# Two-block network on one core: experts gather the unsplit h and sum in a tile apart, h g + b moves to the last eight experts, one more weight buffer, GpSimd products on VectorE

## Chip, cores and metric

One core of a Trainium2 chip runs the whole kernel. The metric is the device time of one execution in microseconds. The profiled execution is one of these executions.

## The reference

Two blocks of two layers each, on 256 tokens of width 1024, all in float32. The first block puts 16 meta tokens ahead of the 256 and has a gated linear recurrence in its first layer and a short convolution in its second; each is followed by a layer norm and by a mixture of 32 experts, of which every token takes two. The second block has a state space layer and an attention layer, each followed by a dense layer of width 4096.

```python
# layer i of the first block
mixed = rglru_mixer(h, ...) if i == 0 else shortconv_mixer(h, ...)
h = layer_norm(ALPHA * h + mixed, ln_g[i, 0], ln_b[i, 0])      # (x - mu) * rsqrt(var) * g + b
ffn = hierarchical_moe(h, ...)     # router: best of 4 groups, best two of its 8 experts, gates
h = layer_norm(ALPHA * h + ffn, ln_g[i, 1], ln_b[i, 1])
# one expert: (silu(x @ w_gate[e]) * (x @ w_up[e])) @ w_down[e], 1024 -> 512 -> 1024
```

The 32 experts of one layer hold 201 MB of weights, all of which are read.

## The kernel before

The 256 tokens live in two tiles `h[0]` and `h[1]` of 128 x 1024 (token on the partition). After a norm the tile holds only (x - mu) * rsqrt(var); the factor g (times ALPHA) and the summand b are applied later, in two ways: where a product needs h transposed, the transposed copy gets g and b per partition; and the tile itself becomes h g + b at a convenient point, before the next sum goes into it (`affine`, L362, `renew`, L368). `load_gb` (L429) fetches the next g and b: four rows of 2 KB with DMAs of GpSimd's queue into two scratch tiles of the pool `xk` (two buffers, also used by `hh` and `ht` of the experts), and four partition broadcasts on GpSimd.

Dense products run in float32r (one pass of TensorE): both operands are split into a high part (ScalarE copy, L294) and a low part (VectorE subtraction, L295), and three matmuls add up (L506 to L508). `feature_part` (L394) makes the split transposed copy of h for these products; of every two calls one is not "fast", and there the low part of a 128 x 512 tile is a GpSimd subtraction (L427). It is called for two tiles in `features` (layer 1 of the first block, state space layer) and for one tile at the end of three later stages, ten such subtractions in all.

`phase_a` (L566) is the first mixer. Its gates make a product `x * q` of 128 x 544 on GpSimd (L641, four times), and its scan a product of 128 x 272 on GpSimd before each `tensor_tensor_scan` (L688, eight times).

`moe` (L786) is the mixture. In this order of the program: router logits (L761, added at L855), `choose` (L801 to L849, some thirty small operations on VectorE that end in the one-hot tile `on`, L828, and later the gates), the ranks of the tokens by three small matmuls with a triangle and with ones (L880) into `rk`, the largest count (a register that all engines load, because an `If`, L1114, treats overfull experts apart), the places `P` (a 0/1 matrix of 128 tokens x 8 experts x 32 slots, L958), and the gather of eight experts at a time: `P` as the moving operand, h as the weights (L940, L941), to transposed inputs `xg`. For this h is split once (`xh` by ScalarE, `xl` by GpSimd, L865 and L866), four tiles of 128 x 1024, and each product takes two matmuls in float32r. After that split, GpSimd turns h into h g + b (`self.affine(self.gb, nc.gpsimd)`, L893) and loads the next g and b.

Then come eight quads of four experts. Each takes gate and up (L995, four experts beside each other in 32 columns of the array), silu on ScalarE (L1003), the multiply on VectorE (L1004), transposes (L1009), down (L1034), and the way back to the tokens (L1046), which VectorE adds to h (L1058). Every second quad gathers for two. The last quad adds and takes the moments of the norm at once.

Weights come through a ring of buffers of 1 MB each (`fetch`, L449, L462), filled by DMAs of SP's queue in program order; a DMA waits until its buffer has been read. In layer 0 the ring has 16 buffers up to the 33rd step of the stage generator, in layer 1 17 for the first two quads and 7 afterwards, because the tables of the state space layer are made beside the other six quads (`s5_prepare`, on all engines). The ring of 7 stays to the end.

The engines work in order each; the program is put into an order by a scheduler, except where an operation is pinned to the order of the program (`self.pin`).

```python
xh = [X.tile([128, KD, 128], F32R, name=f"xh{n}") for n in range(2)]
xl = [X.tile([128, KD, 128], F32R, name=f"xl{n}") for n in range(2)]
for n in range(2):
    src = h[n].rearrange("t (p k) -> t k p", k=KD)
    self.pin(a.copy)(xh[n], src)
    nc.gpsimd.tensor_tensor(xl[n], src, xh[n].bitcast(F32), op=OP.subtract)
```

## Time and profile before

| | us |
|---|---|
| median of 3 runs | 1877.05 (1873.78 to 1881.48) |
| profiled execution, its own time | 1877.19 |
| its span, first to last instruction | 1875.5 |
| TensorE matmuls busy | 1562.1 (83%) |
| VectorE busy | 855.2 (46%) |
| ScalarE busy | 508.0 (27%) |
| GpSimd busy | 177.5 (9%) |

The mean granted clock of TensorE is 0.932 of 2.4 GHz. The kernel reads 526 MB from memory, 281 GB/s over the span. The shares are averages over stages with different limits; a stage is read from its own stretch. An operation's busy time includes the time in which it waits inside the engine for something that is no semaphore.

### The profile page before, as it was taken

The numbers are of one execution on the slowest core, as the hardware profiler recorded it, in microseconds if no ns is written. First come the engines' busy times: TensorE is split into PE (matmuls) and PEld (weight loads), VectorE is DVE, ScalarE is ACT, GpSimd is POOL, SyncE is SP. The second block draws the span as 40 slices with busy tenths as digits, with TensorE's granted clock in tenths as the row PEclk, the third lists the DMA queues.
The fourth block names the chain that finished last, engine by engine and source line by source line (L and its number), as shares of the span: only waits on it lengthen the run. The fifth ranks groups of instructions, "written<-read, shape, count | busy, mean of one in ns | idle before, by whom it ended". The sixth has DMA issues, their size and how long they took to land.

```text
span 1875.5 us, 24906 instructions
## 1 busy us (share of the span) xinstructions
PE 1562.1 (83%) x10036; PEld 996.9 (53%) x10044; DVE 855.2 (46%) x1752; ACT 508.0 (27%) x811; POOL 177.5 (9%) x235
## 2 busy tenths in 40 slices
PE   7878677777777997876787778768999999999997
PEld 6764222211222894221132233247989998879997
DVE  5873111201111966111441342178775657885655
ACT  4631000100000542110010010033554445654442
POOL 3331000000000403001000000012110100310100
PEclk9878989988999998998898899878999999999999
DMA  9356999999999863999999899995745543435530
GB/s 308 141 215 273 420 420 420 420 420 420 419 420 387 305 236 146 421 415 397 399 380 379 339 390 404 357 190 158 248 136 180 188 160 115 167 113 180 180 135 23
DMA packets 150520, 535.56 MB, mean 286 GB/s; under 512 B 23141, under 2 KB 35686, under 8 KB 120698
## 3 DMA queue, kind: packets, MB, share of 16 engines
q1 hardware_dynamic: 148226, 532.04, 75.2%
q0 software_dynamic: 1856, 1.75, 0.4%
q8 instruction: 81, 1.33, 0.3%
q14 instruction: 45, 0.37, 0.1%
q10 hardware_dynamic: 312, 0.07, 0.0%
HBM read 526.49 MB, written 1.05 MB: 281 GB/s over the span
## 4 chain that ended last, share of the span: by engine, by line
PE 35%; DMA 14%; DVE 7%; ACT 2%; POOL 1%; issue 1%; SPq 0%; DVEq 0%; ACTq 0%; POOLq 0%
DMA raw<-in_moe_w_up 9%; PE mm L507 5%; PE mm L506 5%; PE mm L508 5%; PE tp L507 3%; PE tp L506 3%; PE tp L508 3%; DMA raw<-in_moe_w_gate 3%; PE mm L1034 3%; PE mm L995 3%; DMA raw<-in_moe_w_down 2%; PE tp L1449 1%; PE mm L1046 1%; PE mm L1521 1%; DVE hc L1567 0%
## 5 line engine op out<-in xcount | busy, mean ns | idle before, releaser
L995 PE MATMUL mm<-raw,xg 128*32 128x512 f32 x2048 | 381.3, 690 | 164.1 <-DMA raw<-in_moe_w_up 93.1
L295 DVE TENSOR_TENSOR wlo<-raw,whi 128x1024 fp32r<-128x1024 f32 (+3 forms) x265 | 283.7, 1086 | 170.2 <-ACT whi L294 169.5
L995 PEld LDWEIGHTS mm<-raw,xg 128*32 128x32 f32 x2048 | 80.7, 121 | 448.1 <-DMA raw<-in_moe_w_up 170.5
L294 ACT CAST whi<-raw 128x1024 fp32r<-128x1024 f32 (+3 forms) x265 | 239.0, 917 | 245.3 <-PE mm L508 100.1
L1004 DVE TENSOR_TENSOR hh<-hh,mm 128x512 f32<-128x512 f32 x16 | 11.0, 688 | 470.3 <-PE mm L995 470.3
L1034 PE MATMUL mm<-raw,ht 128*32 128x512 f32 (+2 forms) x1120 | 208.6, 604 | 17.0 <-DMA raw<-in_moe_w_down 12.1
L506 PE MATMUL mm<-whi,f 128*128 128x512 f32 (+3 forms) x432 | 150.0, 347 | 0.0
L507 PE MATMUL tp<-f,whi 128*128 128x256 f32 x512 | 146.4, 286 | 4.2 <-DVE f L423 4.2
L507 PE MATMUL mm<-wlo,f 128*128 128x512 f32 (+3 forms) x432 | 149.8, 347 | 0.0
L508 PE MATMUL mm<-whi,f 128*128 128x512 f32 (+3 forms) x432 | 149.1, 346 | 0.0
L506 PE MATMUL tp<-f,whi 128*128 128x256 f32 x512 | 146.3, 286 | 0.4 <-ACT f L417 0.4
L508 PE MATMUL tp<-f,wlo 128*128 128x256 f32 x512 | 146.1, 286 | 0.0
L1034 PEld LDWEIGHTS mm<-raw,ht 128*32 128x32 f32 x1120 | 53.7, 118 | 129.5 <-issue 84.9
L1003 ACT ACTIVATE hh<-mm 128x512 f32<-128x512 f32 x16 | 9.6, 597 | 416.2 <-PE mm L995 416.1
L507 PEld LDWEIGHTS tp<-f,whi 128*128 128x128 f32 x512 | 99.7, 195 | 4.5 <-issue 4.5
L506 PEld LDWEIGHTS tp<-f,whi 128*128 128x128 f32 x512 | 99.5, 195 | 1.3 <-ACT f L417 0.9
L508 PEld LDWEIGHTS tp<-f,wlo 128*128 128x128 f32 x512 | 99.8, 195 | 0.0
L507 PE MATMUL mm<-xl,whi 128*128 128x272 f32 (+2 forms) x320 | 93.1, 292 | 0.8 <-DVE xl L295 0.4
L506 PE MATMUL mm<-xh,whi 128*128 128x272 f32 (+2 forms) x320 | 92.8, 295 | 0.6 <-ACT yg L678 0.4
L508 PE MATMUL mm<-xh,wlo 128*128 128x272 f32 (+2 forms) x320 | 92.1, 289 | 0.0
L506 PEld LDWEIGHTS mm<-whi,f 128*128 128x128 f32 x432 | 81.8, 189 | 10.3
L508 PEld LDWEIGHTS mm<-whi,f 128*128 128x128 f32 x432 | 81.5, 189 | 10.1 <-DVE f L423 0.2
(615 smaller groups left out, 2425.5 us busy)
## 6 DMA issues: line engine op xcount, KB each, us to landing
raw<-in_moe_w_gate SPq DMA_DIRECT2D x128, 1024.0 KB, 12.3
raw<-in_moe_w_up SPq DMA_DIRECT2D x128, 1024.0 KB, 19.9
raw<-in_moe_w_down SPq DMA_DIRECT2D x120, 1024.0 KB, 19.0
raw<-in_w_ff SPq DMA_DIRECT2D x64, 1024.0 KB, 4.9
raw<-in_sc_w_in SPq DMA_DIRECT2D x12, 1024.0 KB, 12.4
raw<-in_lru_w_in SPq DMA_DIRECT2D x8, 1024.0 KB, 13.8
raw<-in_ssm_w_glu SPq DMA_DIRECT2D x8, 1024.0 KB, 10.5
raw<-in_moe_w_down SPq DMA_DIRECT2D x12, 512.0 KB, 13.3
```

What stands on the lines that cost most here:

```text
L294: f(self.nc.scalar.copy)(hi, src)
L295: f(self.nc.vector.tensor_tensor)(lo, src, hi.bitcast(F32), op=OP.subtract)
L506: mm(out, lhsT=lh, rhs=rh, start=first, stop=False, skip_group_check=shared)
L507: mm(out, lhsT=lh, rhs=rl, start=False, stop=False, skip_group_check=shared)
L508: mm(out, lhsT=ll, rhs=rh, start=False, stop=last, skip_group_check=shared)
L995: nc.tensor.matmul(gu[m][i * 32:(i + 1) * 32, :], lhsT=xg[hf][:, k, c], rhs=wgu[hf * n + part][m][i][:, k % (4 // n), :], start=hf == 0 an ...
L1003: a.activation(hh, gu[0], AF.Silu)
L1004: v.tensor_tensor(hh, hh, gu[1], op=OP.mult)
L1034: nc.tensor.matmul(o[e * 32:(e + 1) * 32, :], lhsT=ht[:, j, e * 32:(e + 1) * 32], rhs=w[e], start=j == 0, stop=j == 3)
L1046: nc.tensor.matmul(o, lhsT=pt[:, n, :], rhs=y[c.start // 512][j][:, c.start % 512:(c.stop - 1) % 512 + 1], start=j == 0, stop=j == 1)
L1449: nc.tensor.matmul(po[:, :, j:4, :], lhsT=sel[:, 67 - 64 * g - j:195 - 64 * g - j], rhs=Kg[:, g, :, 0:4 - j, :], start=n == 0, stop=n == 7)
L1521: nc.tensor.matmul(p, lhsT=self.place[:, 128 * q4 + 3 - j:128 * q4 + 131 - j], rhs=x[:, :, 64 * j:64 * j + 64], start=j + i == 0, stop=j + ...
```

## The change

- The gather takes h itself (`hk`, a view of the tiles) in plain f32, one matmul instead of two; `xh` and `xl` are gone, with the copies and subtractions that made them, and `P` is f32.
- The experts' results are added into two new tiles `acc`, cleared by GpSimd at the start of `moe`, instead of into h. In quad 6, after its gate and up products are issued, `renew` turns h into h g + b on VectorE and loads the next g and b, and VectorE adds `acc` to h; quads 6 and 7 add to h as before.
- In layer 0 the router of the two meta rows (`lg2`, `choose`) and the cleared tile `yo` move behind the first gate and up products.
- The subtraction of `feature_part`, the gates' product and the scan's product go from GpSimd to VectorE.
- The ring has one buffer more: 17 instead of 16 in layer 0, 8 instead of 7 from the third quad of layer 1 on. Two places give room for it: the scan tiles `hc` of the state space layer use a second buffer of the ring, and the value tile `vv` of the attention is one.

```diff
     def renew(self, key, scale=None):
-        self.affine(self.gb)
+        for z in self.h:
+            for t, op in zip(self.gb, (OP.mult, OP.add)):
+                self.pin(self.nc.vector.tensor_tensor)(z, z, t, op=op)
         self.gb = self.load_gb(key, scale)
...
             a.copy(dst[0][:, s, o], y)
-            nc.gpsimd.tensor_tensor(dst[1][:, s, o], y, dst[0][:, s, o].bitcast(F32), op=OP.subtract)
+            v.tensor_tensor(dst[1][:, s, o], y, dst[0][:, s, o].bitcast(F32), op=OP.subtract)
...
-                    nc.gpsimd.tensor_tensor(x, x, q, op=OP.mult)
+                    v.tensor_tensor(x, x, q, op=OP.mult)
...
-                nc.gpsimd.tensor_tensor(x, x, tt[:, t, :], op=OP.mult)
+                v.tensor_tensor(x, x, tt[:, t, :], op=OP.mult)
...
+            acc = [X.tile([128, D], F32, name=f"acc{n}") for n in range(2)]
+            for t in acc:
+                nc.gpsimd.memset(t, 0.0)
...
-            xh = [X.tile([128, KD, 128], F32R, name=f"xh{n}") for n in range(2)]
-            xl = [X.tile([128, KD, 128], F32R, name=f"xl{n}") for n in range(2)]
-            for n in range(2):
-                src = h[n].rearrange("t (p k) -> t k p", k=KD)
-                self.pin(a.copy)(xh[n], src)
-                nc.gpsimd.tensor_tensor(xl[n], src, xh[n].bitcast(F32), op=OP.subtract)
...
-            self.affine(self.gb, nc.gpsimd)
-            self.gb = self.load_gb(("a", layer, 1))
...
+            hk = [t.rearrange("t (p k) -> t k p", k=KD) for t in h]
...
-                            nc.tensor.matmul(o, lhsT=xh[n][:, k, :], rhs=P[n], start=n == 0, stop=False)
-                            nc.tensor.matmul(o, lhsT=xl[n][:, k, :], rhs=P[n], start=False, stop=n == 1)
+                            nc.tensor.matmul(o, lhsT=hk[n][:, k, :], rhs=P[n], start=n == 0, stop=n == 1)
...
-                    t = B.tile([128, 8, 32], F32R, name=f"P{n}")
+                    t = B.tile([128, 8, 32], F32, name=f"P{n}")
...
+                if qd == 6:
+
+                    self.renew(("a", layer, 1))
+                    for n in range(2):
+                        v.tensor_tensor(h[n], h[n], acc[n], op=OP.add)
+                    acc = h
                 if N == 3 and qd == 0:
+                    lg2 = S.tile([2, 1, 36], F32, name="lg2")
+                    v.tensor_tensor(lg2[:, 0, :], self.logits(layer, self.x2[:, 0]), self.br[layer][:2, :], op=OP.add)
+                    gt2 = choose(lg2, "2")[1]()
...
-                            v.tensor_tensor(h[n][:, c], h[n][:, c], back(n, c), op=OP.add)
+                            v.tensor_tensor(acc[n][:, c], acc[n][:, c], back(n, c), op=OP.add)
...
-            t = self.fetch(None, [128, 4, 8, 64])
+            t, u = (self.fetch(None, [128, 4, 8, 64]) for _ in range(2))
...
-                hcs.append([keep.tile([128, 8, 64], F32, name=f"hc{i}{n}") if i else t[:, 2 + n] for n in range(2)])
+                hcs.append([keep.tile([128, 8, 64], F32, name=f"hc{n}") if i == 3 else (t[:, 2:], u, u[:, 2:])[i][:, n] for n in range(2)])
...
-            vv = P.tile([128, 2, NH, 128], F32, name="vv")
+            vv = self.fetch(None, [128, 2, NH, 128])
...
         self.shrink()
-        self.grow(1)
+        self.grow(2)
...
         self.grow(4, AT)
-        self.grow(2)
+        self.grow(3)
         self.moe(0, [128, 128, 2], self.stages0())
```

The loop over overfull experts adds to `acc` in the same way; it isn't entered with these inputs.

## Rows read from the trace of the kernel before

**Rows 1.** Windows view: stretch in us, busy us by engine, granted clock, DMA share, GB/s

```profile
80.00:92.00 12.00, 4.80 (x12) 3.26 (x13) 9.54 (x17) 9.56 (x17) 8.31 (x6) 0.61 0.01 1
140.00:158.00 18.00, 14.09 (x99) 7.88 (x104) 11.42 (x63) 2.82 (x5) 4.22 (x6) 0.79 0.16 51
160.00:570.00 410.00, 312.14 (x1638) 97.77 (x1638) 59.67 (x129) 27.07 (x43) 0.95 (x1) 0.94 1.01 420
726.00:748.00 22.00, 12.62 (x77) 7.79 (x81) 12.94 (x33) 1.33 (x3) 11.14 (x8) 0.65 0.02 7
960.00:1170.00 210.00, 163.44 (x992) 61.28 (x994) 63.77 (x117) 19.41 (x32) 0.98 (x2) 0.92 0.97 375
1020.00:1060.00 40.00, 35.66 (x204) 14.55 (x202) 15.96 (x27) 3.79 (x6) 0.00 (x0) 0.93 0.83 291
```

**Rows 2.** Groups of VectorE by line, 125 to 139 us: busy us, mean ns

```profile
L811 DVE TENSOR_TENSOR goh<-goh,rev 128x8 f32<-128x8 f32 x1 | 2.8, 2786 | 0.0
L828 DVE TENSOR_TENSOR on<-oh,oh 128x64 f32<-128x64 f32 x1 | 2.2, 2246 | 0.0
L817 DVE TENSOR_TENSOR els<-lg,gof 128x64 f32<-128x64 f32 x1 | 2.2, 2244 | 0.0
L813 DVE TENSOR_TENSOR goh<-goh,gsm 128x8 f32<-128x8 f32 x1 | 2.1, 2066 | 0.0
L837 DVE TENSOR_TENSOR g<-m 128x2 f32<-128x2 f32 x1 | 1.6, 1629 | 0.0
L810 DVE TENSOR_TENSOR goh<-lg,gmx 128x8 f32<-128x8 f32 x1 | 1.2, 1191 | 0.0
...
L827 DVE TENSOR_TENSOR oh<-iota,i 128x64 f32<-128x64 f32 x1 | 0.2, 212 | 0.0
```

**Rows 3.** Timeline around the router of layer 0: start us, us

```profile
123.56 5.68 POOL L866 TENSOR_TENSOR xl<-h,xh 128x1024 fp32r<-128x1024 f32 x2 [31.89 <-ACT xh L96]
129.20 9.54 POOL L96 TENSOR_TENSOR h<-h,gb 128x1024 f32<-128x1024 f32 x4
152.11 0.15 DVE L810 TENSOR_TENSOR goh<-lg,gmx 2x4 f32<-2x4 f32 x1
```

**Rows 4.** Timeline of TensorE, layer 0, from the ranks to the first gate product

```profile
138.88 0.64 PE L880 MATMUL mm<-on,tri 128*128 128x32 f32 x2 [10.37 <-DVE on L828]
...
151.37 1.07 PE L995 MATMUL mm<-raw,xg 128*32 128x512 f32 x3
```

**Rows 5.** Timeline around the router of layer 1

```profile
719.64 2.44 DVE L810 TENSOR_TENSOR goh<-lg,gmx 128x8 f32<-128x8 f32 x1
732.22 2.25 DVE L828 TENSOR_TENSOR on<-oh,oh 128x64 f32<-128x64 f32 x1
```

**Rows 6.** Timeline of TensorE: split gather, and plain f32 products of the same shape

```profile
160.91 0.28 PE L940 MATMUL tp<-P,xh 128*128 128x256 f32 x1
...
161.14 0.28 PE L940 MATMUL tp<-P,xh 128*128 128x256 f32 x1
...
1631.57 0.59 PE L1873 MATMUL mm<-kz,qt 128*128 128x256 f32 x2
1632.00 0.59 PE L1896 MATMUL mm<-e,vv 128*128 128x256 f32 x2
```

**Rows 7.** First block: VectorE's wait (us in total, times, longest), and its scans

```profile
DVE rq L642 <- POOL xc L641: 4.9, 4, 1.2
...
71.99 2.43 DVE L689 TENSOR_TENSOR_SCAN tt<-rq,xc 128x272 f32<-128x272 f32 x2 [0.87 <-POOL xc L688]
92.24 1.33 DVE L689 TENSOR_TENSOR_SCAN tt<-rq,xc 128x272 f32<-128x272 f32 x2
```

**Rows 8.** Groups of GpSimd by line: the feature subtraction

```profile
L427 POOL TENSOR_TENSOR f<-xk,f 128x512 fp32r<-128x512 f32 x8 | 11.0, 1376 | 114.2 <-ACT f L426 84.9 <-issue 29.3
```

**Rows 9.** Groups by line: the experts' multiply with its idle time, the broadcast

```profile
L1004 DVE TENSOR_TENSOR hh<-hh,mm 128x512 f32<-128x512 f32 x16 | 11.0, 688 | 470.3 <-PE mm L995 470.3
L444 POOL PARTITION_BROADCAST gb<-gbr x32 | 38.8, 1303 | 205.6 <-DVE h L96 184.2 <-SPq L1114 12.1 <-ACT xh L294 8.3
```

More of the change, by code (lines that the diff above doesn't have):

```diff
@@ L360, in norm, with renew @@
         self.norm_end(small, n)
-    def affine(self, gb, e=None):
+    def renew(self, key, scale=None):
         for z in self.h:
-            for i, op in enumerate((OP.mult, OP.add)):
-                self.pin((e or self.nc.vector).tensor_tensor)(z, z, gb[i], op=op)
-    def renew(self, key, scale=None):
-        self.affine(self.gb)
+            for t, op in zip(self.gb, (OP.mult, OP.add)):
+                self.pin(self.nc.vector.tensor_tensor)(z, z, t, op=op)
         self.gb = self.load_gb(key, scale)
@@ L869, in moe @@
             logits(1)
+            next(two, None)
             if N == 2:
                 self.warm(WARMR)
-            next(two, None)
             on, gates = choose(lg, "")
@@ L969, in moe @@
             with self.pool("mz") as Z:
-                self.moe_rest(layer, S, B, Z, nc.values_load(most), counts, rk, gt, gather, cap)
-            if N == 3:
-                lg2 = S.tile([2, 1, 36], F32, name="lg2")
-                v.tensor_tensor(lg2[:, 0, :], self.logits(layer, self.x2[:, 0]), self.br[layer][:2, :], op=OP.add)
-                gt2 = choose(lg2, "2")[1]()
-                yo = X.tile([128, D], F32, name="yo")
-                nc.gpsimd.memset(yo, 0.0)
+                self.moe_rest(layer, S, B, Z, nc.values_load(most), counts, rk, gt, gather, cap, acc)
             for qd in range(8):
@@ L998, in moe @@
                         next(stages, None)
+                if qd == 6:
[3 more added lines that the diff above has]
+                    acc = h
                 if N == 3 and qd == 0:
+                    lg2 = S.tile([2, 1, 36], F32, name="lg2")
+                    v.tensor_tensor(lg2[:, 0, :], self.logits(layer, self.x2[:, 0]), self.br[layer][:2, :], op=OP.add)
+                    gt2 = choose(lg2, "2")[1]()
                     next(two)
                     affine2(1, *self.f_ln["a", layer, 0])
+                    yo = X.tile([128, D], F32, name="yo")
+                    nc.gpsimd.memset(yo, 0.0)
                 hh = self.scratch("hh")
@@ L1016, in moe @@
                 for n in range(2):
-                    nc.tensor.transpose(p[:, n * 128:(n + 1) * 128], P[n].bitcast(F32)[:, q], self.ident)
+                    nc.tensor.transpose(p[:, n * 128:(n + 1) * 128], P[n][:, q], self.ident)
                 o = p[:, 256:260]
                 for n in range(2):
-                    nc.tensor.matmul(o, lhsT=P[n].bitcast(F32)[:, q], rhs=gt[:, n, e0:e0 + 4], start=n == 0, stop=n == 1 and N == 2)
+                    nc.tensor.matmul(o, lhsT=P[n][:, q], rhs=gt[:, n, e0:e0 + 4], start=n == 0, stop=n == 1 and N == 2)
                 if N == 3:
@@ L1108, in most, with moe_rest @@
         return mi, counts
-    def moe_rest(self, layer, S, B, Z, most, counts, rk, gt, gather, cap):
-        nc, I, tc, h = self.nc, self.I, self.tc, self.h
+    def moe_rest(self, layer, S, B, Z, most, counts, rk, gt, gather, cap, acc):
+        nc, I, tc = self.nc, self.I, self.tc
         v, a = nc.vector, nc.scalar
@@ L1132, in chunk @@
                             v.tensor_scalar(s, re[:, n:n + 1], -cap - 64.0 * c, None, op0=OP.add)
-                            t = Z.tile([128, 64], F32R, name=f"P{n}")
+                            t = Z.tile([128, 64], F32, name=f"P{n}")
                             v.tensor_scalar(t, self.iota, s, None, op0=OP.is_equal)
                             g = Z.tile([128, 64], F32, name=f"Pg{n}")
-                            v.tensor_scalar(g, t.bitcast(F32), ge[:, n:n + 1], None, op0=OP.mult)
+                            v.tensor_scalar(g, t, ge[:, n:n + 1], None, op0=OP.mult)
                             q = self.bank("tp")
@@ L1167, in chunk @@
                                 nc.tensor.matmul(o, lhsT=pt[:, n, :], rhs=y[i], start=True, stop=True)
-                                v.tensor_tensor(h[n][:, cc], h[n][:, cc], o, op=OP.add)
+                                v.tensor_tensor(acc[n][:, cc], acc[n][:, cc], o, op=OP.add)
                     chunk(0)
```

## The prediction

> **What bounds the kernel now.** I read the windows view first. From 160 to 570 us, the expert loop of layer 0, the DMA engines are busy all the time at 420 GB/s while TensorE is busy 312 of 410 us [rows 1]: that stretch is paid by bytes, and only an earlier start of the stream, or more bytes ahead of it, shortens it. Then I looked for the places where the stream stands still. There are two holes in front of the expert loops, 140 to 158 us (DMA share 0.16) and 726 to 748 us (0.02) [rows 1]: all weight buffers are full and nothing is consumed yet, because the router has not chosen. A third stretch, 1020 to 1060 us, runs at 291 GB/s with TensorE busy 35.7 of 40 us [rows 1]; there TensorE is late. After 1205 us the dense blocks are bound by TensorE and the DMA doesn't matter.
>
> So the question is what fills the holes. The groups of VectorE in the router of layer 0 show six small two-input products, 128x2 to 128x64 elements, of 1191 to 2786 ns [rows 2]. The same line on a 2x4 tile, without a neighbour on GpSimd, takes 0.15 us [rows 3]. The timeline gives the cause: GpSimd runs two subtractions (5.68 us) and four products (9.54 us) at that time [rows 3], and each of the six ends where one of these ends. TensorE waits 10.37 us for the last of them [rows 4]. Layer 1 repeats it: six such products, the first 2.44 us, the last 2.25 us, the last ends at 734.47 [rows 5].
>
> **The sum.** It is made against the profiled execution: 1877.2 us, span 1875.5, its median neighbour 1877.05, so they can be taken as one. A measurement of this kernel tells about 0.5%, 9.4 us, from no change.
>
> *Router of layer 0.* The change takes away the ScalarE copies, the GpSimd subtractions and the four products from here. The six add up to 1191 + 2786 + 2066 + 2244 + 1629 + 2246 = 12.16 us [rows 2]; free, 6 x 0.18 = 1.1 us (between the 0.15 of the 2x4 product [rows 3] and the 0.21 of an unhindered 128x64 one [rows 2]). That is 11.1 us, but TensorE waited only 10.37 [rows 4], so 10.4. The partition broadcasts of the next g and b, 1.3 us each [rows 9], leave too, and the 2-row router moves behind the first gate and up products (about 1 us of TensorE and VectorE together). Against it stands the gather: unsplit, a pair of matmuls (high, low) becomes one. The pair starts every 161.14 - 160.91 = 0.23 us; an unsplit f32 product of the same 128x256 shape every 1632.00 - 1631.57 = 0.43 us [rows 6]. Half a gather is 8 of them: +1.6 us. Net 11 us; bounds 9 (nothing besides the six, gather wholly exposed) and 12.
>
> *One buffer more.* 128 x 2048 x 4 bytes = 1.05 MB, at 420 GB/s [rows 1] 2.5 us of stream that runs before the consumer comes. The hole of layer 0 is (1 - 0.16/1.01) x 18 = 15.1 us; 11 + 2.5 = 13.5 still fits into it, so both count. The Trainium skill (DMA: Bandwidth & Descriptors, Where 436 GB/s comes from) lets the memory side bind a load at about 358 GB/s; by that the buffer would be worth 2.9 us (an estimate from that figure), but the trace streams at 420 and the measurement decides.
>
> *Router of layer 1.* Six products at 13.4 us by the same pattern (the first and last are in [rows 5]), less 1.1: 12.3. The split gather ran 16 matmuls at 1.2 GHz here (granted clock 0.65 over the hole [rows 1]); an unsplit one at 2.4 GHz takes as long, 8 x 0.43 = 3.5 us, and at 1.2 GHz 7 us. I take 12; bounds 8.5 and 13. The hole, 22 us, is longer than that. The first eight experts have 17 buffers before and after; the new one comes only after them.
>
> *Inside layer 1.* From 960 to 1170 us the stream gives 375 GB/s [rows 1], against 420 a loss of 210 x 45/420 = 22 us, over half of it (40 x 129/420 = 12 us) in 1020 to 1060. Seven buffers become eight there: 2.5 us for each time the consumer falls behind, some four times at most, 10 us. But two of the later pairs of quads gather in this stretch, 2 x 2 halves x 1.6 = 6.4 us on an engine that is late. Bounds -6.4 and +10; +2, since where TensorE is busy 35.7 of 40 us a buffer pays once.
>
> *First block.* Four products 128x544 and eight 128x272 go from GpSimd to VectorE. VectorE waited 4.9 us for the former [rows 7], and its scans beside the latter took 2.43 us for two instead of 1.33 [rows 7]. On VectorE they cost about 0.7 us (a 128x512 product: 688 ns [rows 9]) and half of it: 4 x 0.72 + 8 x 0.4 = 6 us. Only 80 to 92 us counts, where TensorE is busy 4.8 of 12 us [rows 1]; half of the waits (2.5) and the scans' and subtractions' delay (some 2.5) lie there, and half of the new work (3). +2, bounds 0 and 3.5.
>
> *The ten feature subtractions* cost 1376 ns on GpSimd [rows 8], about 0.7 on VectorE [rows 9], each in front of a projection. But VectorE now waits in order for ScalarE's copy, and behind it stand the scaling of the next tile and its statistics, for which TensorE's transposes wait. +1 in all; bounds -2 and +4.
>
> *The quad before the last* (qd 6) takes over h g + b: four products and two sums of 128x1024, each at most twice 688 ns [rows 9], 8 us per layer on VectorE, in front of the multiply of gate and up. Before that multiply VectorE idles 470 us over 16 quads, 29 each [rows 9], so they cost nothing; without that cover, 8 us per layer. Behind them GpSimd loads the next g and b (four small DMAs of its own queue, four broadcasts of 1.3 us) into the two scratch buffers that the multiply and its transposed copy use next; that ends some 8 + 5 = 13 us after the last gather of the quad, still inside the 29. Clearing the two new sums is a GpSimd write before the router; nobody waits for it until the first sum. The GpSimd and SP queues have nothing else behind these steps. The shared scan buffers and the attention's value tile in the ring cost 0, between -1 and +4 (a buffer held longer).
>
> Sum: 11 + 2.5 + 12 + 2 + 2 + 1 = 30.5. 1877.2 - 30.5 = 1847 us, own range 1836 to 1858.
>
> **Rivals.** *Something else is late next* (0.17). With VectorE free, sixteen small matmuls of the meta rows, the branch that all engines pass before the loop, and a gather still at 1.2 GHz stand between router and first product. Then layer 0 gives 7, layer 1 8.5, the first block 2, and the stretch inside layer 1 loses 4: 13.5, so 1864 us. For it: between 138.88 and the first product at 151.37 [rows 4] lie 12.5 us that the change hardly touches. Against it: that stretch exists before, too, so it delays nothing anew.
>
> *All covers hold and the buffers pay fully* (0.12): 15 in the first hole, 13, 8, 3.5 and 3 make 42.5, so 1835 us. Against it: TensorE is busy where the eighth buffer would pay.
>
> *The unsplit gather binds* (0.04, slower). Place: all 16 half gathers, on TensorE. Price: 1.6 us each at 2.4 GHz, 25 us if all are exposed, less than the gain; at 1.2 GHz 3.2 each, 51 us, so 1877 - 30 + 51 = 1898 us. It decides once more than 30 of these 51 lie on the path. Against it: granted clock 0.94 over 160 to 570 us and 98 us of idle TensorE there [rows 1]. The Trainium skill (TensorE: Matmul & The Clock Gate, Loop structure matters more than you think) holds that a loop which waits for DMA between its matmuls lets TensorE run cold, which would feed this rival. By that rule the estimate is those 1898 us; the clock of 0.94 bears it out only in part.
>
> *It doesn't do what it says* (0.01): the order of the engines puts h g + b back ahead of the router, and the time stays at 1875.
>
> **How the numbers follow.** Forecast 0.66, rivals 0.17, 0.12, 0.04, 0.01. The range 1833 to 1862 holds nearly all of the first, under half of the second, most of the third: about 0.8. Faster by over 0.5% (below 1867.7): 0.66 + 0.14 + 0.12 = 0.92; same 0.05 (the tail of the second, and the last); slower 0.03.
>
> **What would show it.** Right: the six products at about 0.2 us, VectorE's router about 3 us long, the first hole nearly gone, the second at some 10 us, the first gate product of layer 0 about 13 us earlier and of layer 1 about 25; L295-like subtractions of 0.7 us in place of GpSimd's; VectorE's h g + b in the idle time before the multiply of qd 6. Wrong: a hole that keeps its length with another releaser behind it; a first product that still starts some 25 us after the router's logits; TensorE at the half clock in the gathers; a multiply of qd 6 that waits for a broadcast; a stream below 375 GB/s inside layer 1.

## The result, and the profile after

The changed kernel takes 1858.34 us (median of 4 runs, 1848.97 to 1861.03) against 1879.26 for the kernel before beside it: ratio 0.9866, 95% interval 0.984 to 0.9891. The two medians lie 20.9 us apart; the ratio, which is taken over all runs and is not that of the medians, makes 25.2 us of the 1877.05 us of the table above (20.5 to 30.0 by its interval). 30.5 were forecast. The first trace is that of the longest of the four runs (1861.03 us, span 1859.1), so a second trace (`again`, below) stands beside it wherever it matters.

The page of the first trace: busy time by engine, and GB/s in 40 slices.

```profile
PE 1583.7 (85%) x10036; PEld 1025.0 (55%) x10044; DVE 844.3 (45%) x1786; ACT 500.0 (27%) x807; POOL 123.8 (7%) x205
...
GB/s 305 148 210 354 420 420 420 419 420 420 410 420 384 308 211 293 420 411 390 409 377 344 375 369 362 367 141 176 252 138 199 185 142 108 159 136 182 185 111 23
```

TensorE is busy 21.6 us longer than before (1583.7 against 1562.1). The windows view, in the stretches of [rows 1]:

```profile
80.00:92.00 12.00, 7.48 (x24) 6.00 (x24) 11.12 (x26) 8.79 (x16) 0.00 (x0) 0.72 0.01 2
140.00:158.00 18.00, 14.30 (x97) 7.11 (x98) 1.72 (x4) 1.59 (x2) 1.34 (x2) 0.81 0.64 251
160.00:570.00 410.00, 321.16 (x1637) 106.57 (x1636) 68.31 (x156) 26.94 (x44) 9.06 (x9) 0.93 1.01 419
726.00:748.00 22.00, 20.86 (x168) 10.00 (x164) 2.73 (x8) 4.88 (x6) 0.00 (x0) 1.00 1.00 408
960.00:1170.00 210.00, 168.25 (x942) 65.75 (x942) 58.53 (x102) 16.71 (x28) 6.94 (x8) 0.88 0.94 368
1020.00:1060.00 40.00, 30.37 (x192) 10.92 (x194) 17.23 (x34) 6.06 (x10) 0.97 (x2) 1.00 0.95 365
```

The hole at 140 to 158 us moves 251 GB/s instead of 51, that at 726 to 748 us 408 instead of 7. Inside layer 1 the stream of this trace is slower than before: 368 instead of 375 GB/s from 960 to 1170 us; in `again` it is 378. So the gain is made in front of the loops, and the first trace gives part of it back inside the second. VectorE in the router of layer 0, timeline, the answer to [rows 2]:

```profile
123.34 0.17 DVE L811 TENSOR_TENSOR goh<-lg,gmx 128x8 f32<-128x8 f32 x1
...
123.54 0.17 DVE L812 TENSOR_TENSOR goh<-goh,rev 128x8 f32<-128x8 f32 x1
...
124.34 0.23 DVE L818 TENSOR_TENSOR els<-lg,gof 128x64 f32<-128x64 f32 x1
...
125.69 0.22 DVE L829 TENSOR_TENSOR on<-oh,oh 128x64 f32<-128x64 f32 x1
```

The products of 1.2 to 2.8 us are 0.17 to 0.23 us long, as forecast. TensorE from the ranks to the first gate product, in layer 0 and in layer 1 (the answer to [rows 4, 5]):

```profile
126.51 0.62 PE L874 MATMUL mm<-on,tri 128*128 128x32 f32 x2
...
130.58 5.64 PE L933 MATMUL tp<-P,h 128*128 128x256 f32 x16
...
143.70 9.14 PE L981 MATMUL mm<-raw,xg 128*32 128x512 f32 x64 [6.18 <-DVEq L1111]
...
713.30 0.38 PE L874 MATMUL mm<-on,tri 128*128 128x32 f32 x2 [0.38 <-DVE den L840]
...
715.14 4.18 PE L933 MATMUL tp<-P,h 128*128 128x256 f32 x16
...
721.40 4.07 PE L981 MATMUL mm<-raw,xg 128*32 128x512 f32 x36 [0.79 <-PEq L1111]
```

The same two places of layer 1 in the kernel before:

```profile
734.61 0.61 PE L880 MATMUL mm<-on,tri 128*128 128x32 f32 x2 [12.62 <-DVE den L839]
...
743.69 7.07 PE L995 MATMUL mm<-raw,xg 128*32 128x512 f32 x64 [0.77 <-PEq L1114]
```

In layer 0 the ranks start 12.37 us earlier than in [rows 4] (126.51 against 138.88), the first gate product only 7.67 (143.70 against 151.37): 6.18 us are spent waiting for VectorE's sequencer at the branch (L1111). In layer 1 the first gate product starts 22.3 us earlier (721.40 against 743.69). Groups by line, the answer to [rows 8, 9]:

```profile
L423 DVE TENSOR_TENSOR f<-xk,f 128x512 fp32r<-128x512 f32 x8 | 6.2, 776 | 0.5 <-ACT f L422 0.4
...
L1001 DVE TENSOR_TENSOR hh<-hh,mm 128x512 f32<-128x512 f32 x16 | 11.0, 688 | 423.4 <-PE mm L981 399.2 <-issue 24.2
```

The feature subtraction costs 776 ns on VectorE instead of 1376 on GpSimd and waits for ScalarE 0.4 us in all. In front of the experts' multiply VectorE still idles 423 us in all, 399 of them for TensorE, so h g + b in the seventh quad had its cover.

The lead over the kernel before, taken at the same operation of each trace (us; the kernel before has one trace). The first reduction is `gmx`, the first operation of `choose`; from it to the one-hot tile `on` is called the choice below. The multiply is VectorE's product of silu and up, one per quad; half a gather is eight products (16 matmuls in the trace, split or not).

| from ... to | forecast | first trace | `again` |
|---|---|---|---|
| start to the router's first reduction in layer 0 | 2 | 1.9 | 4.0 |
| to the first gate product of layer 0 | 11 | 5.8 | 5.8 |
| to the first reduction in layer 1 | 2.5 | 1.4 | 1.6 |
| to the first gate product of layer 1 | 12 | 13.2 | 13.5 |
| to the last multiply of layer 1 | 2 | -7.6 | -0.9 |
| to the end | 1 | 1.6 | 1.9 |
| sum, before rounding | 30.5 | 16.3 | 25.7 |

Two terms failed: the way out of the router of layer 0, and the inside of layer 1. The experiments go after these two, and after the cause of the gain. Where times of different groups of runs are compared, it is by the ratio to the kernel before, whose median moved between 1879 and 1883 us.

### The profile page after: what moved, and what is told of

The parts are those of the page before. It is cut to its first block, busy times and chain, and to the rows that moved or that the text cites. A ratio compares the mean times of both kernels' runs of the same rounds, so it can differ in the third digit from the quotient of the medians.

```text
span 1859.1 us, 24869 instructions
## 1 busy us (share of the span) xinstructions
PE 1583.7 (85%) x10036; PEld 1025.0 (55%) x10044; DVE 844.3 (45%) x1786; ACT 500.0 (27%) x807; POOL 123.8 (7%) x205
## 4 chain that ended last, share of the span: by engine, by line
PE 38%; DMA 13%; DVE 6%; ACT 2%; issue 1%; POOL 1%; SPq 0%; DVEq 0%; ACTq 0%; POOLq 0%
DMA raw<-in_moe_w_up 9%; PE mm L503 5%; PE mm L502 5%; PE mm L504 5%; PE mm L1031 4%; PE tp L503 3%; PE tp L502 3%; PE tp L504 3%; PE mm L981 3%; DMA raw<-in_moe_w_gate 2%; DMA raw<-in_moe_w_down 2%; PE tp L1446 2%; PE tp L933 1%; PE tp L1432 1%; DVE h L96 0%
## 5 line engine op out<-in xcount | busy, mean ns | idle before, releaser
L981 PE MATMUL mm<-raw,xg 128*32 128x512 f32 x2048 | 367.9, 684 | 152.7 <-DMA raw<-in_moe_w_up 86.9
L1031 PE MATMUL mm<-raw,ht 128*32 128x512 f32 (+2 forms) x1120 | 205.8, 603 | 14.7 <-DMA raw<-in_moe_w_down 11.1
```

Of the source, the lines that this page charges most:

```text
L981: nc.tensor.matmul(gu[m][i * 32:(i + 1) * 32, :], lhsT=xg[hf][:, k, c], rhs=wgu[hf * n + part][m][i][:, k % (4 // n), :], start=hf == 0 an ...
L1031: nc.tensor.matmul(o[e * 32:(e + 1) * 32, :], lhsT=ht[:, j, e * 32:(e + 1) * 32], rhs=w[e], start=j == 0, stop=j == 3)
```

## The experiments

**One part alone.** From the kernel before:

```diff
-                nc.gpsimd.tensor_tensor(xl[n], src, xh[n].bitcast(F32), op=OP.subtract)
...
             on, gates = choose(lg, "")
             next(two, None)
+            for n in range(2):
+                src = h[n].rearrange("t (p k) -> t k p", k=KD)
+                self.pin(v.tensor_tensor)(xl[n], src, xh[n].bitcast(F32), op=OP.subtract)
...
-            self.affine(self.gb, nc.gpsimd)
-            self.gb = self.load_gb(("a", layer, 1))
...
+                if qd == 0:
+                    self.renew(("a", layer, 1))
```

> The kernel before with one part of the change alone: GpSimd is taken off the router. h g + b and the loading of the next g and b move behind the first gate and up products, on VectorE; the low part of the split h is a VectorE subtraction behind the one-hot tile. The split gather, the sums in h, 16 and 7 buffers, and the products of GpSimd elsewhere stay. Theory A, the router carries nearly all of the gain and the unsplit gather gives some back: six small products at 0.2 us, ranks some 10 us earlier in each layer, first gate product at 141 to 143 us in layer 0 and 19 to 22 us earlier in layer 1, half gathers 2 us; no loss in the last quads of layer 1; time 1855 to 1860 us, as fast as the whole change. Theory B, buffers, unsplit gather and the moved sum carry a good half of it: 1864 to 1868 us.

Measured: ratio 0.9889 (0.9865 to 0.9913), 1858.18 us. From the first reduction to the one-hot tile 2.77 us in layer 0 (13.77 before) and 3.45 in layer 1 (15.02 before); first gate products at 142.84 and 724.90, 8.5 and 18.8 us earlier. Theory A holds: by the ratios, of the 25 us about 21 come from the router alone (the intervals of this kernel and the changed one overlap). No loss in the last quads of layer 1 (below). Here, and in own_copy, split_vec and split_8, the sums of the loop over overfull experts, which isn't entered, would be scaled too.

**GpSimd beside the router.** The changed kernel, with work added where the two sum tiles are cleared:

```diff
                 nc.gpsimd.memset(t, 0.0)
+            for n, t in [(0, acc[0]), (1, acc[1])] * 3:
+                if N == 3:
+                    nc.gpsimd.tensor_tensor(t, t, h[n], op=OP.mult)
+                else:
+                    nc.gpsimd.tensor_scalar(t, h[n], 0.0, None, op0=OP.mult)
```

> The changed kernel with work added on GpSimd while the router chooses: in layer 0 six two-input products of 128x1024 (a cleared sum tile times h, so the sum stays zero), in layer 1 six one-input products of the same size (h times 0.0). Theory A, a small two-input product of VectorE waits for a two-input one of GpSimd to end, and for nothing else of GpSimd: in layer 0 the six products take 1.2 to 2.8 us again and the one-hot tile is done some 13 us after the logits instead of 2.8; in layer 1 they stay at 0.2 us and it is done 2.8 us after the logits. Theory B, any stream of GpSimd through the tiles' memory does it: both layers are stretched alike. Theory C, it was the ScalarE copies or the order, and neither layer changes.

Measured: 1869.27 us, one run. In layer 0 the one-hot tile is done 11.3 us after the first reduction instead of 2.77. The timeline of VectorE, with GpSimd's row:

```profile
121.02 0.49 DVE L816 TENSOR_TENSOR goh<-lg,gmx 128x8 f32<-128x8 f32 x1
...
121.55 2.29 DVE L817 TENSOR_TENSOR goh<-goh,rev 128x8 f32<-128x8 f32 x1
...
124.07 2.07 DVE L819 TENSOR_TENSOR goh<-goh,gsm 128x8 f32<-128x8 f32 x1
...
126.17 2.27 DVE L822 TENSOR_SCALAR gof<-goh 128x8 f32<-128x8 f32 x1
...
128.48 2.32 DVE L823 TENSOR_TENSOR els<-lg,gof 128x64 f32<-128x64 f32 x1
...
131.91 0.23 DVE L834 TENSOR_TENSOR on<-oh,oh 128x64 f32<-128x64 f32 x1
...
116.82 13.89 POOL L803 TENSOR_TENSOR acc<-acc,h 128x1024 f32<-128x1024 f32 x6
```

GpSimd's six products (2.3 us each) end at 130.71; each slow operation of VectorE ends when one of them does, and what starts after 130.71 is fast again. That shows what made the choice long, and so the cause of most of the gain. In layer 1 GpSimd began its one-input products at 723.8, after the choice, so that half told nothing. It was repeated in layer 0, with eight of them:

```diff
+            for n, t in [(0, acc[0]), (1, acc[1])] * 4:
+                if N == 3:
+                    nc.gpsimd.tensor_scalar(t, h[n], 0.0, None, op0=OP.mult)
```

> The changed kernel with eight one-input products on GpSimd in layer 0 (h times 0.0 into the cleared sum tiles, 2.8 us each), from before the logits to behind the one-hot tile; gpsimd_load had them in layer 1, where they began only after the choice. Theory A, only a two-input product of GpSimd holds VectorE up: the products of the choice stay at 0.2 us, the one-hot tile is done 2.8 us after the first reduction. Theory B, any stream of GpSimd does: products of 1 to 2.8 us, one-hot tile after 11 us or more.

Measured: 1857.32 us, one run; the same view:

```profile
123.42 0.17 DVE L814 TENSOR_TENSOR goh<-lg,gmx 128x8 f32<-128x8 f32 x1
...
124.22 0.60 DVE L820 TENSOR_SCALAR gof<-goh 128x8 f32<-128x8 f32 x1
...
124.86 1.02 DVE L821 TENSOR_TENSOR els<-lg,gof 128x64 f32<-128x64 f32 x1
...
127.00 0.22 DVE L832 TENSOR_TENSOR on<-oh,oh 128x64 f32<-128x64 f32 x1
...
119.23 21.98 POOL L803 TENSOR_SCALAR acc<-h 128x1024 f32<-128x1024 f32 x8
```

GpSimd is busy through the whole choice, and it costs VectorE 1.2 us, on two operations, instead of 8.5. Theory A holds but for this rest. The Trainium skill (SBUF — State Buffer, Who interferes with whom) states that a VectorE instruction with two SBUF inputs contends with a GpSimd instruction that reads SBUF, and that the port pair which the two share is locked for one of them at a time. The two-input run agrees. The one-input run doesn't for the most part: those products read SBUF too, and most of VectorE's products beside them kept their 0.17 to 0.23 us; here the measurement decides.

**The changed kernel again, and TensorE's clock.** No edit.

> The changed kernel itself, for a second trace. In the first one TensorE ran at a granted clock of 0.50 from 1136 to 1146 us, in the last quad but one of layer 1, where eight down products took 3.63 us instead of 1.91, and that quad and the next lost about 10 us of the 24.9 us gained up to there. Theory A, a matter of the single execution: another trace has these products at 1.9 us, the lead over the kernel before still above 20 us at the last silu, and a span of 1850 to 1855 us. Theory B, it belongs to the kernel's order (more TensorE work for the gather in front of it): the half clock is there again, the lead falls below 17 us, span 1858 to 1862 us.

Measured: ratio 0.9856 (0.9834 to 0.9877), 1854.77 us; the profiled run spans 1849.7. Theory A. The windows view from the multiply of the last quad but one to that of the last, the same 290 matmuls, of the first trace:

```profile
1121.40:1189.00 67.60, 54.95 (x290) 19.82 (x290) 9.63 (x20) 3.14 (x5) 0.00 (x0) 0.82 0.96 374
```

and of `again`:

```profile
1117.90:1179.80 61.90, 48.12 (x290) 16.82 (x290) 9.67 (x20) 3.14 (x5) 0.00 (x0) 0.94 1.03 407
```

At a granted clock of 0.82 this stretch takes 67.6 us, at 0.94 61.9: 5.7 of the 9.4 us between the two spans. In the first trace TensorE was busy all ten microseconds from 1136 to 1146 us at 0.50 (1.2 GHz), after 8.62 of ten at 0.75. Over all traces the stretch takes 61.6 to 63.0 us at 0.89 to 0.94, in the kernel before too, and 65.5 to 68.2 at 0.82 to 0.90. `pad`, `products_back` and `split_8` below have 0.82 there, so a span of one trace alone is no verdict here. The mean clock is not all of it: one_input took 62.0 us at 0.89, ring_less 65.5 at 0.90. Why the clock is lower in some executions stays open.

**The buffer, and the order of the gather's weights.** First the changed kernel without the new buffers:

```diff
-        self.grow(2)
+        self.grow(1)
         self.tables_now = False
...
-        self.grow(3)
+        self.grow(2)
         self.moe(0, [128, 128, 2], self.stages0())
```

> The changed kernel with one weight buffer fewer in both layers (16, and 7 after the second quad of layer 1), as before the change. Theory A, the buffer is worth little: in layer 0 the weights stop landing 2.5 us earlier, and since VectorE's instructions after the branch come in only behind them, the first gate product starts at 141 instead of 143.7 us; entry of layer 1 within 1 us of the changed kernel, inside layer 1 up to 4 us lost; time 0 to 5 us above the changed kernel, 1856 to 1862 us. Theory B, the buffer pays in full: first gate product still at 143.7, 2.5 us later out of layer 0 and 10 us later out of layer 1, 1868 to 1872 us.

Then, on top of it:

```diff
+            hk = [X.tile([128, KD, 128], F32, name=f"hk{n}") for n in range(2)]
+            for n in range(2):
+                self.pin(a.copy)(hk[n], h[n].rearrange("t (p k) -> t k p", k=KD))
...
-            hk = [t.rearrange("t (p k) -> t k p", k=KD) for t in h]
```

> As ring_less, and the room of the buffer goes to a copy of h in the order that the gather reads (ScalarE, two copies of 128x1024 in front of the router), so that the gather's weights lie side by side instead of 32 bytes apart. Theory A, the pace of the gather is set by the loading of these weights (337 ns each, against 190 ns for the attention's f32 weights): a weight load takes 190 ns, a matmul of the gather starts every 0.215 us instead of 0.266, a half gather takes 3.4 us instead of 4.3, and time falls 3 to 6 us below ring_less, since half of layer 1's gathers lie where TensorE is late. Theory B, the pace is set by the four passes of an f32 product: half gather 4.3 us as before, same time as ring_less within 2 us.

Measured: ring_less 0.9906 (0.9877 to 0.9935), 1864.42 us; contig 0.9905 (0.9882 to 0.9928), 1862.69 us. By the ratios the buffers are worth 0.4 to 0.5%, 7.5 to 9.4 us, between A (up to 5) and B (some 12 more), though the intervals of ring_less and the changed kernel overlap or just touch. The first gate product of ring_less stayed at 143.72, which speaks against A's reason as well. The groups of the gather's weight loads, changed kernel (min/median/max ns):

```profile
L933 PEld LDWEIGHTS tp<-P,h x256: 312/337/338, 130.5 to 1073.8; 128*128 128x128 f32 x128
```

contig:

```profile
L935 PEld LDWEIGHTS tp<-P,hk x256: 186/190/337, 128.6 to 1076.1; 128*128 128x128 f32 x128
```

So weights read 32 bytes apart load in 337 ns, side by side in 190, as theory A of contig said. One half gather of layer 1, which other matmuls interrupt, in the changed kernel, in contig, and the first and last rows of both its parts in the kernel before:

```profile
1058.63 0.85 PE L933 MATMUL tp<-P,h 128*128 128x256 f32 x2 [0.24 <-ACT BL L1412]
1061.25 3.73 PE L933 MATMUL tp<-P,h 128*128 128x256 f32 x14
...
1062.05 0.70 PE L935 MATMUL tp<-P,hk 128*128 128x256 f32 x2 [0.24 <-ACT BL L1414]
1064.52 3.29 PE L935 MATMUL tp<-P,hk 128*128 128x256 f32 x14
...
1081.84 0.39 PE L940 MATMUL tp<-P,xh 128*128 128x256 f32 x1 [0.24 <-ACT BL L1415]
...
1082.31 0.28 PE L941 MATMUL tp<-P,xl 128*128 128x256 f32 x1
...
1084.36 0.39 PE L940 MATMUL tp<-P,xh 128*128 128x256 f32 x1
...
1085.78 0.29 PE L941 MATMUL tp<-P,xl 128*128 128x256 f32 x1
```

A half gather's 16 matmuls take 0.85 + 3.73 = 4.58 us in the changed kernel and 0.70 + 3.29 = 3.99 in contig; the 16 of the split gather took 0.75 + 1.71 = 2.46 in the kernel before. Against the changed kernel contig gains 0.6 us per half gather, not the 0.9 that A had, and the time of the whole kernel didn't fall with it, as theory B had it.

**What layer 1 gives back.** Three more kernels complete the picture: own_copy (17 and 8 buffers, contiguous unsplit copies in the room of the sums), split_vec (router_only with the three kinds of products on VectorE), split_8 (the same with eight buffers in layer 1). From the first multiply of layer 1 to the seventh (the last quad is left out, because of the clock):

| gather | 7 buffers | 8 buffers |
|---|---|---|
| split, two matmuls | 379.8 (before), 379.3, 378.9 | 373.6 |
| unsplit, side by side | 384.8 | 383.9 |
| unsplit, 32 bytes apart | 388.3 | 381.5, 380.6, 388.3, 383.8, 384.4, 383.7 (mean 383.7) |

(One trace each; the last row has the changed kernel twice, and meta_back, products_back, pad and one_input, which share its gather and buffers there. gpsimd_load does too, with its added products of GpSimd at the start of the stretch: 387.8.) The six traces of the last field, of kernels that don't differ there, lie 7.7 us apart, so a difference of a few us between two single traces is not shown. Read with that in mind, with seven buffers the unsplit gather costs 9 us, 5.5 if its weights lie side by side. Six half gathers lie in this stretch, at 4.58 - 2.46 = 2.1 us more each: 12.7 us, of which 9 show. The eighth buffer gives 1 to 5.5. The changed kernel has both and by the mean loses 3.9 us.

own_copy, its core (the meta router also stands where it did before):

```diff
-            acc = [X.tile([128, D], F32, name=f"acc{n}") for n in range(2)]
...
+            hk = [X.tile([128, KD, 128], F32, name=f"hk{n}") for n in range(2)]
+            for n in range(2):
+                self.pin(a.copy)(hk[n], h[n].rearrange("t (p k) -> t k p", k=KD))
...
-                if qd == 6:
+                if qd == 0:
                     self.renew(("a", layer, 1))
-                    for n in range(2):
-                        v.tensor_tensor(h[n], h[n], acc[n], op=OP.add)
-                    acc = h
```

> As meta_back, and without the sums apart: h is copied by ScalarE into the order that the gather reads (unsplit, f32), in the room of the two sum tiles; h g + b moves to VectorE behind the first gate and up products, and the experts add to h. 17 and 8 buffers. The sums of the loop over overfull experts, which isn't entered, would then be scaled too. Theory A, TensorE's time in the gathers is what layer 1 gives back: a half gather takes 3.5 us instead of 4.3, layer 1 keeps its lead up to the last silu within 2 us, time 3 to 6 us below meta_back. Theory B, the place of the gather's time doesn't matter once there is an eighth buffer (contig gained nothing over ring_less): as meta_back within 2 us.

Measured: 0.9832 (0.98 to 0.9863), 1850.37 us; 0.2% (3.0 us by the medians) below meta_back (under the wait at the branch), which the intervals don't separate. Between first and last multiply of layer 1 445.8 us against 449.9 in meta_back and 442.8 in the kernel before. Where nothing interrupts it, its half gather took 3.7 us against 4.2 in meta_back (theory A had 3.5 and 4.3). Between the two theories the runs don't decide.

split_vec and split_8:

```diff
-            nc.gpsimd.tensor_tensor(dst[1][:, s, o], y, dst[0][:, s, o].bitcast(F32), op=OP.subtract)
+            v.tensor_tensor(dst[1][:, s, o], y, dst[0][:, s, o].bitcast(F32), op=OP.subtract)
...
-                    nc.gpsimd.tensor_tensor(x, x, q, op=OP.mult)
+                    v.tensor_tensor(x, x, q, op=OP.mult)
...
-                nc.gpsimd.tensor_tensor(x, x, tt[:, t, :], op=OP.mult)
+                v.tensor_tensor(x, x, tt[:, t, :], op=OP.mult)
```

> router_only with the gates' product, the scan's product and the feature subtraction on VectorE too: split gather, 16 and 7 buffers, no sums apart. (A token of the loop over overfull experts, which isn't entered, would be scaled wrongly.) Theory A, the split gather keeps layer 1's loop at 442 to 443 us, the products give 2 us in the first block and 2 after the last silu: 4 to 5 us below router_only, 1850 to 1853 us, level with the changed kernel with one buffer fewer. Theory B, the products cost as much elsewhere as they give: as router_only within 1 us.

Measured: 0.9839 (0.9815 to 0.9864), 1852.78 us, theory A in time; the gain over router_only is 5.4 us by the medians and 0.5%, 9.4 us, by the ratios, where 4 to 5 us were expected.

```diff
-                    t = B.tile([128, 8, 32], F32R, name=f"P{n}")
+                    t = B.tile([128, 8, 32], F32R, name=f"P{n}", bufs=1)
...
-        self.grow(1)
+        self.grow(2)
         self.tables_now = False
```

> split_vec with eight weight buffers instead of seven from the third quad of layer 1 on (16 in layer 0 as before); the room comes from single tiles for the places P and for pt, and from the shared scan tiles and the value tile in the ring as in the changed kernel. Theory A, inside layer 1 the time of the gather on TensorE and the eighth buffer each count: first gate product of layer 1 to the last multiply takes 436 to 438 us, against 440.7 in split_vec and 450 in the changed kernel, time 3 to 4 us below split_vec, 1846 to 1849 us. Theory B, with the split gather the buffer has nothing left to cover: 440 us and the time of split_vec within 1 us, 1852 us.

Measured: 0.981 (0.9781 to 0.9839), 1849.92 us. The first seven quads are 5.3 us shorter than in split_vec, more than A asked; then the last quad ran at 0.82 and took 66.0 us instead of 61.8, so that the whole loop, first to last multiply, took 439.6 (440.7 in split_vec by the same count, which is the one that the expectation's numbers follow). By the median of the runs, and by its trace up to there, it is the fastest kernel of the study, some 0.5% below the changed kernel; the intervals just touch.

**The products on VectorE.** The changed kernel with the three kinds of products on GpSimd again (the reverse of the diff of split_vec):

> The changed kernel with the gates' product, the scan's product and the feature subtraction on GpSimd again. Theory A, these moves pay a little: router logits of layer 0 1 to 3 us later, from the last silu to the end 2 to 3 us longer (the lead over the kernel before stays as it is there instead of growing by 2), time 3 to 5 us above the changed kernel, 1854 to 1857 us. Theory B, they are covered: within 1 us of the changed kernel at both places.

Measured: 0.9888 (0.986 to 0.9917), 1860.19 us, 4 to 6 us above the changed kernel by the ratios, as theory A has it, but the intervals overlap. First reduction at 123.85 us, against 123.14 and 121.03; that alone tells little, since in the other kernels that have these products on VectorE it lies anywhere between 120.8 and 124.0. From the last multiply to the end 672.6 us, against 670.2 and 669.9, and 671.8 before. This part is clearer: the three kernels with the subtraction on GpSimd need 671.7 to 672.6 us, the eleven with it on VectorE at most 671.2. And one thing that no theory had: the wait at the branch of layer 0 is gone.

**The wait at the branch.** In the changed kernel VectorE takes the branch at 138.1 us and goes on at 143.6; in layer 1 at 719.8 and 720.4 (first and last start, VectorE's sequencer):

```profile
L1111 DVEq EVENT_SEMAPHORE  x4: 21/21/21, 143.6 to 720.4; - x4
...
L1111 DVEq COMPARE_BRANCH  x2: 63/68/72, 138.1 to 719.8; - x2
```

In products_back 137.8 and 138.4:

```profile
L1111 DVEq EVENT_SEMAPHORE  x4: 21/21/21, 138.4 to 720.1; - x4
...
L1111 DVEq COMPARE_BRANCH  x2: 63/68/72, 137.8 to 719.4; - x2
```

Windows view of the wait, changed kernel: no engine works, the weights stream:

```profile
138.10:143.60 5.50, 0.00 (x0) 0.00 (x0) 0.00 (x0) 0.00 (x0) 0.00 (x0) 0.77 1.00 405
```

and the DMA view of the same stretch, packets and MB of the queues that bring instructions:

```profile
q8 instruction: 1, 0.02, 1.2%
q14 instruction: 2, 0.02, 0.7%
```

The first guess was the new place of the meta router, the second the address of the code behind the branch.

```diff
+            if N == 3:
+                lg2 = S.tile([2, 1, 36], F32, name="lg2")
...
             for qd in range(8):
...
-                    lg2 = S.tile([2, 1, 36], F32, name="lg2")
```

> The changed kernel with the router of the two meta rows and the clearing of yo in front of the expert loop again, as before the change. In the changed kernel VectorE goes on 5.6 us after the branch of layer 0, in the kernel before and in router_only 0.6 us, in layer 1 0.6 us everywhere. Theory A, the new place of that router is what makes VectorE's instructions late: it goes on 0.6 us after the branch, the first gate product of layer 0 starts at 138 to 140 us instead of 142 to 144, the hole of 5 us in the weight stream there shrinks to 2, time 2 to 4 us below the changed kernel, 1847 to 1850 us. Theory B, the wait comes from weights in flight (the stream still ran when VectorE reached the branch): still 5 us, time 0 to 1 us above the changed kernel.

```diff
+            if N == 3:
+                for i in range(4):
+                    v.memset(S.tile([128, 1], F32, name=f"pad{i}"), 0.0)
             self.route(1, B.tile([128, KD, 128], F32, name="xg", bufs=2))
```

> The changed kernel with four writes of one element per partition on VectorE ahead of the router of layer 0, nothing else. VectorE executes 304 instructions up to the branch in the kernels where it goes on 5 to 5.6 us later, 293, 296, 298 and 307 in those where it goes on after 0.6; the changed kernel has twelve more than products_back. Theory A, it is where the code behind the branch lies: at some places the next piece of VectorE's code is asked for only after the branch, and its fetch then runs beside the weight stream. With four instructions more VectorE goes on after 0.6 us, the first gate product starts some 14 us behind the one-hot tile instead of 17.8, the hole in the weight stream there shrinks from 5 to 2 us, time 2 to 4 us below the changed kernel, 1848 us. Theory B, VectorE waits there for another engine: still 5 us, same time as the changed kernel.

Measured: meta_back 0.9851 (0.9827 to 0.9875), 1853.39 us, wait 5.5 us, first gate product at 143.54. pad 0.9842 (0.9817 to 0.9868), 1854.75 us, wait 5.5 us, first gate product at 143.06. Both guesses, as put, fall. What the traces show: the wait is 5.0 to 5.6 us in seven traces of the changed kernel and its relatives (the changed one twice, ring_less, contig, meta_back, pad, one_input), 0.6 in the kernel before, router_only, own_copy, products_back, split_vec and split_8. In gpsimd_load, where the branch came after the last weight had landed, it is 2.9:

```profile
L1116 DVEq EVENT_SEMAPHORE  x4: 21/21/21, 146.1 to 725.3; - x4
...
L1116 DVEq COMPARE_BRANCH  x2: 63/68/72, 143.2 to 724.6; - x2
```

In this one trace the wait without the stream is thus about half as long, but the stream alone isn't the cause: router_only and products_back took their branch with the stream running, at 410 GB/s, in 0.6 us. All kernels that wait have both the sums apart and the twelve products of the first block on VectorE; own_copy and split_vec have the products without the sums, products_back the sums without the products, and none of these waits. The Trainium skill (Runtime: NRT & Kernel Launch, Instruction fetch mechanics) states that a taken branch whose target isn't in the two pages at hand has to fetch the target by DMA before the engine goes on. That fits the instruction packets in the wait, and so does their timing: by the packet records, VectorE goes on 1.62 to 1.65 us after the last packet of q14 in the wait has landed in six of the seven traces, 2.0 us after it in contig. But packets of q14 land 1 to 4 us behind the branch in products_back and own_copy too, where VectorE doesn't wait, and which page was at hand no run here shows. The cause is left open. So is what the wait costs: products_back, without it, enters layer 1 (first reduction) 9.4 us ahead of the kernel before, the changed kernel 9.1 and 11.4.

## Why the prediction was right, and where it wasn't

**The cause of the gain was right.** The six products went from 12.16 us [rows 2] to 0.2 us each; the choice became 11.0 us shorter in layer 0 (10.4 to 11.1 forecast) and 12.25 in layer 1 (12.3 forecast). router_only gives some 21 of the 25 us (by the ratios), and gpsimd_load brings the slow products back.

**The way out of the router of layer 0: 11 forecast, 5.8 measured.** The step that failed is that behind the one-hot tile the sum has only the gather's +1.6 and some 2 us back for broadcasts and meta router, and puts the branch at nothing. Up to VectorE's branch the net was 0.9 us more (11.26 us from the one-hot tile before, 12.16 after). In that, the half gather went from 2.77 to 5.64 us, nearly twice the 1.6: the ranks ran at 1.2 GHz (granted clock 0.50 from 126 to 130 us) and the gather at a mean of 0.67. From the gather's end to the branch 4.3 us became 1.9, about what was forecast. Then the wait at the branch, 0.6 us before, became 5.5. The forecast had the branch among the rivals ("Something else is late next") and dismissed it: "that stretch exists before, too, so it delays nothing anew". That sentence was wrong.

**Layer 1's router: 12 forecast, 13.2 and 13.5 measured.** Besides the choice, ranks and gather ran at 2.4 GHz (granted clock 1.00 from 713 to 720 us; 0.55 from 737 to 742 in the kernel before, where TensorE had waited 12.6 us for the choice). The half gather took 4.18 us, where 3.5 were taken for that clock.

**Inside layer 1: +2 forecast, -7.6 and -0.9 measured.** The sign was wrong, and the ends (-6.4 to +10) missed the first trace. The +2 doesn't follow from its own terms: a buffer that "pays once", 2.5, less 6.4 for the gathers makes -3.9. Two sizes failed besides. The price of the unsplit gather came from [rows 6], f32 products whose weights lie side by side: 0.43 us a product, 1.6 us more per half gather; with weights 32 bytes apart it is 2.1 more. contig, with 3.99 - 2.46 = 1.5, shows that the 1.6 was right for the other order. And only two gathers (four halves, 6.4 us) were counted where TensorE is late; of the six halves between first and seventh multiply, 12.7 us, 9 show in the one trace for that. The buffer gave 1 to 5.5, and the gathers ate more. The rest of the first trace, some 5 us, is its slower last quad, at a granted clock of 0.82 instead of 0.94.

**The buffer of layer 0** paid: the weight stream starts again 7.14 us earlier than in the kernel before (149.42 against 156.56), and the fourth quad's multiply stands 9.5 us earlier, 2.4 more (2.5 forecast). ring_less tests it: with the same start of the first gate product (143.72 and 143.70) and one buffer fewer, that multiply comes at 336.06 instead of 334.20, 1.9 us later.

**First block and subtractions.** 1.9 and 4.0 us for the first block (2 forecast, 0 to 3.5), 1.6 and 1.9 after the last multiply (1 forecast). products_back loses 2.5 to 2.7 us of the second; the first, 0.7 to 2.8, is within what single traces differ by.

**h g + b in the seventh quad** cost nothing visible: the multiply of that quad waited for TensorE alone. VectorE's four products ran earlier than forecast, from 1083.1 us on, three of them ahead of the way back of the sixth quad; there TensorE waited 3.96 us for VectorE, in the kernel before 4.28.

Of the rivals, "Something else is late next" (1864 us) came nearest to what went wrong; the result lies between it and the forecast of 1847. The median of 1858.34 is within the range of 1833 to 1862, but at the end of the forecast's own 1836 to 1858 and nearer to the rival; 25.2 us off 1877.05 by the ratio would be nearer to the forecast. Of the prediction's signs of being wrong, a stream below 375 GB/s inside layer 1 came in the first trace (368) and not in `again` (378), and TensorE stood at the half clock just before the first gather of layer 0.

## What to carry to other kernels

Look at what GpSimd runs beside a chain of small VectorE products: two-input operations of GpSimd stretched six of them from about 0.2 us to 1.2 to 2.8, and taking them out of that stretch gave most of this gain. Price a matmul by a row with the same layout of its weights, not only the same shape; 32 bytes between neighbours cost 147 ns per load here. Before calling an engine's time free because the stage is bound by bytes, look for the stage where that engine is late, and count all of the operation's instances there.

## What was not expected

- After one branch VectorE went on 5.0 to 5.6 us late in some kernels, 0.6 in others, with edits that had nothing to do with the branch (products of other stages moved between engines). Instruction packets land in the wait; in the one trace where no weights were in flight it took 2.9 us.
- A small one-input operation of VectorE (128x8, usually 0.17 us) took 2.27 us beside GpSimd's two-input product, like the two-input ones; in the kernel before it took 0.17 beside such a product.
- The same 290 matmuls of one quad took 61.6 to 63.0 us or 65.5 to 68.2, with a mean granted clock of 0.89 to 0.94 or 0.82 to 0.90, in executions of one and the same kernel too.
